# Spilled activations at every fourth step of the loop over v; the routing's low parts on VectorE, and three expert tiles a turn in its last turns

## The chip, the core and the metric

The kernel runs on one core of a Trainium2 chip. The metric is the device time of one launch in microseconds; the times shown of the kernel before are three runs. The engines: TensorE (PE; PEld its weight loads), VectorE (DVE), ScalarE (ACT), GpSimd (POOL) and SyncE (SP), which issues most transfers. Each engine works through its own queue in order and waits on semaphores for the others.

## The reference

One layer of a hybrid block on 512 tokens of width 1024, all in float32: two token mixers run side by side and are merged into x, then an expert network (PEER) is added, then a last norm. The change touches only the expert network:

```python
q = (tok @ w_q).reshape(n_tok, 8, 2, 128)          # 8 heads, 2 halves
s = einsum('nhpc,hpkc->nhpk', q, sub_keys)         # 128 keys per half
s_top, i_top = top_k(s, 16)
cand = s_top[:, :, 0, :, None] + s_top[:, :, 1, None, :]
best, pos = top_k(cand.reshape(n_tok, 8, 256), 16) # expert = 128 * i + j
gate = softmax(best)
act = gelu(einsum('tkd,td->tk', u[expert], tok)) * gate
out = einsum('tk,tkd->td', act, v[expert])         # 128 experts a token of 16384
```

## The kernel before

The first 128 tokens fetch the rows of u and v that they chose by indirect DMA (`gather`), 128 rows of u and 128 of v; each landed row is one VectorE instruction over 128 x 1024 (`dotu`, then `addv`). The other 384 tokens are done densely: h = gelu(u x) for all 16384 experts, in 128 expert tiles of 128 experts, times a routing weight W that is zero for the experts not chosen, then the product with v. Matrix products are made in three passes (lines 93 to 95): an operand is split into a high part (ScalarE, line 98) and a low part, source minus high part (line 99), by `split`, whose argument `sub` names the engine of the low part.

The order of all of it is written out in the code; there is no planner. A tile of weights goes through `Tiles`: `load` (DMA), `split`, then the matmuls. `H` makes one expert tile: it loads and splits ahead (`feed`: load three tiles ahead, split two ahead), runs 24 matmuls of 384 columns and applies gelu. The first 30 expert tiles (`SPILL`) are written out to DRAM (`dA`) from a ring of three buffers, the next 37 (`AHEAD`) stay in SBUF, and the last 61 are made in the loop over v, into buffers that it has freed.

The stages from 560 us on:

1. Routing, turns n = 0 to 20. A turn makes query tile n (n < 16; `q_mm`, 24 matmuls of 512 columns), its low part (`q_lo`), the scores of half n - 1 (`s_mm`), one to two expert tiles (`H`), the two best-16 searches of half n - 2 (`top_keys`, VectorE), and drives `pairs`, a generator that for each head finds the 16 best of 50 candidate sums and turns their places into expert numbers (VectorE, with the sums on GpSimd); it has five parts, two a turn. `fly` issues gathers for known experts and `land` takes the oldest in. Low parts of query and expert tiles (`wl`) are made by GpSimd here, in the same queue as the candidate sums and the gathers.
2. Transposes of the result, then the W stage: 24 groups, each with four VectorE instructions (`onehot`), 32 matmuls, one landed gather and, in 23 of them, an expert tile. Six more expert tiles follow.
3. The loop over v, steps j = 0 to 127, with 18 matmuls of 512 columns each. `v_load`, `w_load` (every fourth step) and `a_load` (an activation read back from `dA`) issue transfers on SyncE; `v_split` multiplies the activation by W and splits both operands one step ahead. In the first 30 steps every activation is read back and no expert tile is made; from step 30 on each step makes one, until step 90. `pace` spreads the gathers that are left by weights of 11.0 a step, 3.5 less for a step that reads back and 16.5 for an expert tile. Loading of expert tiles beyond the 67th is held back by `cap` during the first steps.

The lines on which the argument turns:

```python
for _ in range(2 if n > 12 else 1 + n % 2):   # expert tiles of turn n, behind s_mm
    H()
...
if hn < NK and hn - AHEAD <= j:               # expert tile in step j over v
    H()
w_load(j + 2)
a_load(j + 2)                                 # if j + 2 < SPILL
```

Of the kernel before, what the change touches and what calls it, by code (L numbers as in the profile page):

```python
# [8 lines left out]
FT = mybir.dt.float32  # L9
# [4 lines left out]
AF = mybir.ActivationFunctionType  # L14
# [11 lines left out]
NK = 128  # L26
# [47 lines left out]
def hybrid_block(ctx: ExitStack, tc: tile.TileContext, A, out, dbg=None):  # L74
    nc = tc.nc
    dbg = dbg or {}
# [62 lines left out]
    with ExitStack() as fr:  # L139
# [425 lines left out]
        for src, dst in ((ig, aT), (F0, eT)):  # L565
            ps = sm.tile([128, TB, 4], FT, name="s")
# [197 lines left out]
    ND = T - NS  # L764
    AHEAD = 37
    NA = 22
    SPILL = dbg.get('spill', 30)
# [2 lines left out]
    TAIL = NK - AHEAD + 8  # L770
    GSCALE = 2.0 ** 14
    RES = dbg.get('res', 6)
    EARLY = dbg.get('early', (1, 1))
    fin = ctx
    fin.enter_context(tc.manual_schedule())
    dA = dram.tile([SPILL, 128, ND], FT, name="dA")
# [3 lines left out]
    iota = pe.tile([128, 128], FT, name="iota")  # L780
# [8 lines left out]
    wqr = pool(rs_, "wqr", 3, reuse_waits="tile")  # L789
# [18 lines left out]
                split(self.f.pop(i), h, l, self.sub)  # L808
                self.p[i] = h, l

    WQ = Tiles((wqr, wqr, wqr), A["w_q_t"], 16, nc.gpsimd, 2)
    qs = {}

    def q_half(n, c, ps):
        h, l = WQ.p[n]
        cs = slice(c * 256, (c + 1) * 256)
# [13 lines left out]

    WQ.load(0)
    WQ.load(1)
    WQ.load(2)
    nc.sync.dma_start(tok0, bcast(A["norm2_row"], D))
    WQ.split(0)
    WQ.split(1)
    first = [rps.tile([128, T], FT, name="q") for _ in range(2)]
# [15 lines left out]
    rings = [pool(fin, "ring" + x, 3, side="right", reuse_waits="tile") for x in "fhl"]  # L853
    ring = pool(fin, "ring", 3, side="right", reuse_waits="tile")
    acts = [pool(fin, "actA", NA, side="right", reuse_waits="tile")]
    U = Tiles(rings, A["u_t"], NK, nc.gpsimd)
    act = {}
    hn = 0

    cap = [AHEAD + SPILL] * 2  # L860
    fed = [3, 2]

    def feed(i):

        while fed[0] < min(cap[0], NK, i + 4):
            U.load(fed[0])
            fed[0] += 1
        while fed[1] < min(cap[1], NK, i + 3):
            U.split(fed[1])
            fed[1] += 1  # L870

    def H():

        nonlocal hn
        i = hn
        hn += 1
        feed(i)
        h, l = U.p.pop(i)
        ps = hps.tile([128, ND], FT, name="h")
        for k in range(KD):  # L880
            mm3(ps, h[:, k], l[:, k], th[:, k, NS:], tl[:, k, NS:], k == 0, k == KD - 1)
        if i < SPILL:
            a = ring.tile([128, ND], FT, name="as", bufs=3)
            nc.scalar.activation(a, ps, AF.Gelu)
            nc.sync.dma_start(dA[i], a)
        else:
            act[i] = acts[(i - SPILL) % AHEAD // NA].tile([128, ND], FT, name="act")
            nc.scalar.activation(act[i], ps, AF.Gelu)  # L888


    def gather(src, j, pl):
# [26 lines left out]
    def land(n):  # L918
        for _ in range(n):
            if flying:  # L920
                f, j, t, pl = flying.pop(0)
                f(j, t)
                room.append(pl)
# [51 lines left out]
    def q_lo(n):  # L975
        ps, qh = qs[n]
        ql = rtt.tile([128, T], FR, name="ql")
        nc.vector.tensor_tensor(ql, ps, qh.bitcast(FT), op=OP.subtract)
        qs[n] = qh, ql
# [101 lines left out]

    U.load(0)
    key_load(0)
    key_load(1)
    U.load(1)
    U.load(2)
    key_split(0)
# [4 lines left out]
    def step():  # L1092
        for g in list(live):
            if next(g, 0) == 0:
                live.remove(g)

    n = 0
    while n < 18 or live:
        WQ.load(n + 3)
        key_load(n + 2)  # L1100
        key_split(n + 1)
        if n < 16:
            q_mm(n)
        WQ.split(n + 2)
        if 1 <= n <= 16:
            s_mm(n - 1)
        for _ in range(2 if n > 12 else 1 + n % 2):
            H()
        t = n - 2
        step()  # L1110
        if 0 <= t < 16:
            top_keys(t, (0, 1))
        fly()
        if n < 16:
            q_lo(n)
        step()
        if 0 <= t < 16:
            top_keys(t, (2, 3))
            if t % 2:
                live.append(pairs(t // 2))  # L1120
        land(EARLY[n % 2])
        n += 1

    flat = lambda t, b: t[:, b].rearrange("p h j -> p (h j)")
# [10 lines left out]
    for n in range(3):  # L1135
        if n == 2:
            H()
        ps = rps.tile([128, ND], FT, name="tr", tag="q" if n % 2 else "s")
# [8 lines left out]
            nc.vector.tensor_tensor(tr[3], gf, tr[2], op=OP.subtract)  # L1147
    nc.vector.tensor_copy(g0, flat(sel[2], 0))
    rs_.close()
    U.sub = nc.vector  # L1150
    acts.append(pool(fin, "actB", AHEAD - NA, reuse_waits="tile"))

    H()
    H()

# [2 lines left out]
    wp = pool(wb, "wb", 1, reuse_waits="tile")  # L1158
    wps = pool(wb, "wps", 5, space=PSUM)
    iota4 = wp.tile([128, 128, 4], HF, name="iota4")  # L1160
    nc.vector.tensor_copy(iota4, iota.unsqueeze(2).to_broadcast([128, 128, 4]))
    GT = 16
    NG = ND // GT
    onehots = {}
# [18 lines left out]
    for g in range(NG):  # L1183
# [9 lines left out]
        for a in range(GT // 4):  # L1193
            ps = wps.tile([128, 4, 128], FT, name="w")
# [32 lines left out]
    def w_load(i):  # L1227
        if i < NK and i % 4 == 0:
            Wt[i // 4] = vp.tile([128, ND // 32, 128], FT, name="W", bufs=2)
            nc.sync.dma_start(Wt[i // 4], dW[i // 4].rearrange("g p x -> p g x"))  # L1230

    def a_load(i):
        if i < SPILL:
            act[i] = ring.tile([128, ND], FT, name="as", bufs=3)
            nc.sync.dma_start(act[i], dA[i])

    def v_split(i):
        if i < NK:
# [18 lines left out]
    PV, PS, PH = dbg.get('pace', (11.0, 3.5, 16.5))  # L1257
# [29 lines left out]
    while hn < AHEAD + SPILL:  # L1287
        H()
        if hn == AHEAD + SPILL - 3:
            v_load(0)  # L1290
            a_load(0)
            w_load(0)
            v_load(1)
            a_load(1)
            nc.sync.dma_start(acc, x1[0:128, :])
        if hn == AHEAD + SPILL - 1:
            v_split(0)
        if hn < AHEAD + SPILL - 2:
            land(1)
            fly()  # L1300
    room.extend([gp] * 3)
    fly()
    xts = {0: acc}
    loaded, parted = 2, 1
    for j in range(NK):
        w = PV - PS * (j < SPILL)
        if SPILL - 12 <= j < SPILL and j % 3 == SPILL % 3:
            cap[0] += 1
            cap[1] += j > SPILL - 12
            feed(hn - 1)  # L1310
        if j == SPILL:
            cap = [NK] * 2
        if hn < NK and hn - AHEAD <= j:
            H()
            w += PH
        while loaded < min(NK, j + (3 if j < TAIL + 3 else 4)):
            v_load(loaded)
            loaded += 1
        w_load(j + 2)
        a_load(j + 2)  # L1320
        while parted < min(NK, j + (2 if j < TAIL + 6 else 3)):
            v_split(parted)
            parted += 1
        pace(w / 2)
        if j < NK - LAST:
            for b in range(ND // 128):
                for c in range(2):
                    VV(j, b, c)
            vparts.pop(j)
        pace(w / 2)  # L1330
        n = j - (NK - 10)
        if n == 0:
            assert not todo and not flying
            nc.sync.dma_start(tok0, bcast(A["final_g"], D))
        if 1 <= n < TB:
            xts[n] = (gp if n == 3 else ga).tile([128, D], FT, name="gat", bufs=3 if n == 3 else 2)
            nc.sync.dma_start(xts[n], x1[n * 128:(n + 1) * 128, :])
# [58 lines left out]
```

## Time and profile before

| | |
|---|---|
| median of three runs | 1892.53 us (1892.1 to 1897.6) |
| profiled execution | 1887.46 us, span 1885.7 us |
| mean granted clock of TensorE | 0.983 |
| TensorE busy | 1805.1 us, 96% |
| VectorE, ScalarE, GpSimd busy | 1372.3, 738.6, 559.3 us |
| transfers | 431.40 MB, mean 229 GB/s |

A busy time is the union of an engine's instructions in a stretch; a matmul's shown duration overlaps that of the next, so the time from one start to the next is what a matmul takes. The stages lie at about 566 to 851 us (routing), 851 to 870 (transposes), 870 to 1062 (W), 1062 to 1082 (six expert tiles), 1082 to 1217 (first 30 steps over v), 1217 to 1717 (steps with expert tiles), and 1717 to the end.

### The profile page before, as it was taken

The page shows a single profiled execution, that of the slowest core. Times are in us where ns is not written, and L with a number is a line of the kernel's source. Part 1 is how long each engine was busy: PE and PEld are TensorE (multiplying, and loading weights), DVE is VectorE, ACT ScalarE, POOL GpSimd, SP SyncE. Part 2 cuts the span into 40 slices and gives each one's busy share as a digit, 9 for nine tenths or more (in the row PEclk, how much of TensorE's full clock was granted, in tenths as well). Part 3 has the DMA queues.
Part 4 walks back from the last instruction along what each step waited for, and adds up shares of the span by engine and source line. Part 5 has one row for each costly group of instructions (what it writes and reads, how often), then busy time and mean ns, then how long its engine had stood idle before and what let it go on. Part 6 is the DMA issues. An engine that isn't in the chain of part 4 may idle for free.

```text
span 1885.7 us, 27396 instructions
## 1 busy us (share of the span) xinstructions
PE 1805.1 (96%) x10281; PEld 1590.1 (84%) x10281; DVE 1372.3 (73%) x2559; ACT 738.6 (39%) x1099; POOL 559.3 (30%) x498
## 2 busy tenths in 40 slices
PE   7999899999999998988999999999999999999998
PEld 6777678887879988888999977899999999998886
DVE  6576673554653799989888476678778877877975
ACT  4565433554334323224444433333333333332433
POOL 0000011100216556462222211155454444444500
PEclk9999999999999999989999999999999999999999
DMA  4446455335625443355888998889999999898982
GB/s 156 133 148 194 134 196 173 113 102 180 228 101 164 150 149 122 126 167 176 270 264 263 307 303 304 301 307 326 323 328 332 325 314 338 310 324 282 374 278 71
DMA packets 242502, 431.40 MB, mean 229 GB/s; under 512 B 22976, under 2 KB 149568, under 8 KB 241344
## 3 DMA queue, kind: packets, MB, share of 16 engines
q1 hardware_dynamic: 143088, 257.66, 40.6%
q0 software_dynamic: 36864, 134.23, 20.5%
q10 hardware_dynamic: 62416, 37.75, 6.7%
q8 instruction: 81, 1.33, 0.3%
q14 instruction: 53, 0.43, 0.1%
HBM read 372.83 MB, written 56.75 MB: 228 GB/s over the span
## 4 chain that ended last, share of the span: by engine, by line
PE 59%; DVE 11%; DMA 4%; issue 1%; ACT 1%; POOL 1%; SPq 0%; DVEq 0%; ACTq 0%; POOLq 0%
PE po L93 8%; PE h L93 8%; PE h L95 8%; PE h L94 8%; PE po L94 8%; PE po L95 8%; PE w L1197 5%; DMA as<-dA 2%; PE m L95 1%; PE m L93 1%; PE m L94 1%; DVE vl L99 1%; DMA vf<-in_v_dram 1%; DVE mr L1001 1%; DVE gat L898 1%
## 5 line engine op out<-in xcount | busy, mean ns | idle before, releaser
L95 PE MATMUL h<-th,wl 128*128 128x384 f32 x1024 | 347.5, 339 | 8.0 <-POOL wl L99 8.0
L93 PE MATMUL h<-tl,wh 128*128 128x384 f32 x1024 | 350.8, 343 | 0.0
L94 PE MATMUL h<-th,wh 128*128 128x384 f32 x1024 | 347.1, 339 | 0.0
L893 POOL DMA_INDIRECT gat<-in_u_dram,eid x128 | 174.8, 1365 | 393.0 <-DVE gat L898 378.9
L93 PE MATMUL po<-vl,ah 128*128 128x512 f32 x654 | 256.9, 393 | 9.0 <-DVE vl L99 9.0
L98 ACT ACTIVATE wh<-wf 128x1024 fp32r<-128x1024 f32 x208 | 218.8, 1053 | 103.2 <-PE m L94 83.0
L94 PE MATMUL po<-vh,ah 128*128 128x512 f32 x654 | 256.2, 392 | 0.0
L95 PE MATMUL po<-vh,al 128*128 128x512 f32 x654 | 255.7, 391 | 0.0
L893 POOL DMA_INDIRECT gat<-in_v_dram,eid x128 | 186.4, 1456 | 209.6 <-DVE acc L904 184.0
L99 DVE TENSOR_TENSOR wl<-wf,wh 128x1024 fp32r<-128x1024 f32 x154 | 188.1, 1222 | 60.7 <-ACT wh L98 60.4
L99 DVE TENSOR_TENSOR vl<-vf,vh 128x1024 fp32r<-128x1024 f32 x111 | 135.9, 1225 | 122.5 <-ACT vh L98 122.1
L888 ACT ACTIVATE act<-h 128x384 f32<-128x384 f32 x98 | 48.2, 492 | 433.1 <-PE h L95 433.1
L95 PEld LDWEIGHTS h<-th,wl 128*128 128x128 f32 x1024 | 195.3, 191 | 8.7 <-POOL wl L99 8.7
L93 PEld LDWEIGHTS h<-tl,wh 128*128 128x128 f32 x1024 | 196.1, 192 | 2.4
L94 PEld LDWEIGHTS h<-th,wh 128*128 128x128 f32 x1024 | 195.8, 191 | 2.3
L99 POOL TENSOR_TENSOR wl<-wf,wh 128x1024 fp32r<-128x1024 f32 x54 | 132.9, 2472 | 112.6 <-ACT wh L98 112.4
L904 DVE SCALAR_TENSOR_TENSOR acc<-gat,dots,acc 128x1024 f32<-128x1024 f32 x128 | 164.1, 1282 | 2.4
L95 PE MATMUL m<-hh,wl 128*128 128x512 f32 (+1 forms) x392 | 154.9, 395 | 9.3 <-DVE wl L99 9.3
L898 DVE SCALAR_TENSOR_TENSOR gat<-gat,tok 128x1024 f32<-128x1024 f32 x128 | 160.0, 1274 | 3.8 <-DMA gat<-in_u_dram,eid 3.8
L93 PE MATMUL m<-hl,wh 128*128 128x512 f32 (+1 forms) x392 | 154.2, 393 | 5.4 <-DVE hl L99 4.2
L94 PE MATMUL m<-hh,wh 128*128 128x512 f32 (+1 forms) x392 | 153.4, 391 | 0.0
L93 PEld LDWEIGHTS po<-vl,ah 128*128 128x128 f32 x654 | 123.4, 189 | 35.5 <-ACT ah L98 11.4
(390 smaller groups left out, 3262.7 us busy)
## 6 DMA issues: line engine op xcount, KB each, us to landing
wf<-in_u_t_dram SPq DMA_DIRECT2D x128, 512.0 KB
vf<-in_v_dram SPq DMA_DIRECT2D x111, 512.0 KB
W<-dW SPq DMA_DIRECT2D x32, 768.0 KB
wf<-in_w_in_t_dram SPq DMA_DIRECT2D x46, 512.0 KB
dW<-stg ACTq DMA_DIRECT2D x11, 2048.0 KB
wf<-in_v_dram SPq DMA_DIRECT2D x17, 512.0 KB
wf<-in_w_q_t_dram SPq DMA_DIRECT2D x16, 512.0 KB
dA<-as SPq DMA_DIRECT2D x30, 192.0 KB
```

The source lines that it names most:

```text
L93: nc.tensor.matmul(ps, lh, rl, start=first, stop=False)
L94: nc.tensor.matmul(ps, lh, rh, start=False, stop=False)
L95: nc.tensor.matmul(ps, ll, rh, start=False, stop=last)
L98: nc.scalar.activation(hi, src, AF.Copy)
L99: (sub or nc.vector).tensor_tensor(lo, src, hi.bitcast(FT), op=OP.subtract)
L888: nc.scalar.activation(act[i], ps, AF.Gelu)
L893: nc.gpsimd.indirect_dma_start(out=t, out_offset=None, in_=src, in_offset=bass.IndirectOffsetOnAxis(ap=eid[:, j:j + 1], axis=0))
L898: nc.vector.scalar_tensor_tensor(t, t, 1.0, tok0, op0=OP.mult, op1=OP.mult, accum_out=dots[:, j:j + 1])
L904: nc.vector.scalar_tensor_tensor(acc, t, dots[:, j:j + 1], acc, op0=OP.mult, op1=OP.add)
L1001: nc.vector.match_replace(r[x], m[:, 0:8], v, -3.0e38)
L1197: nc.tensor.matmul(ps[:, r], og[k][:, a, :, r], O1[:, a, :, r], start=k == 0, stop=k == 1)
```

## The change

Five edits. Query and expert low parts are made on VectorE in the routing too. A turn of the routing makes its expert tiles ahead of the score step instead of behind it, three of them in turns 16 to 20 instead of two; the query's low part comes ahead of the first best-16 search; and no gather is taken in after turn 12. The spilled expert tiles are 0, 4, 8, ..., 116 (`early`) instead of 0 to 29: the expert tiles are made in the order `horder`, the spilled ones first. In the loop over v expert tiles start at step 1 and are spread evenly over 90 steps (`ready`), as far as buffers have been freed; W and activations are loaded three steps ahead instead of two, and `cap` goes. One cast (`iota4`) goes to GpSimd.

```diff
-    WQ = Tiles((wqr, wqr, wqr), A["w_q_t"], 16, nc.gpsimd, 2)
+    WQ = Tiles((wqr, wqr, wqr), A["w_q_t"], 16, nc.vector, 2)
...
-    U = Tiles(rings, A["u_t"], NK, nc.gpsimd)
+    early = [4 * i for i in range(SPILL)]
+    horder = early + [i for i in range(NK) if i not in early]
+    U = Tiles(rings, [A["u_t"][i] for i in horder], NK, nc.vector)
...
-        while fed[0] < min(cap[0], NK, i + 4):
+        while fed[0] < min(NK, i + 4):
...
-            act[i] = acts[(i - SPILL) % AHEAD // NA].tile([128, ND], FT, name="act")
+            a = act[horder[i]] = acts[(i - SPILL) % AHEAD // NA].tile([128, ND], FT, name="act")
...
+        for _ in range(3 if n > 15 else 2 if n > 12 else 1 + n % 2):
+            H()
         if 1 <= n <= 16:
             s_mm(n - 1)
-        for _ in range(2 if n > 12 else 1 + n % 2):
-            H()
         t = n - 2
         step()
+        if n < 16:
+            q_lo(n)
         if 0 <= t < 16:
             top_keys(t, (0, 1))
         fly()
-        if n < 16:
-            q_lo(n)
         step()
...
-        land(EARLY[n % 2])
+        if n < 13:
+            land(1)
...
-    nc.vector.tensor_copy(iota4, iota.unsqueeze(2).to_broadcast([128, 128, 4]))
+    nc.gpsimd.tensor_copy(iota4, iota.unsqueeze(2).to_broadcast([128, 128, 4]))
...
-        if i < SPILL:
+        if i in early:
             act[i] = ring.tile([128, ND], FT, name="as", bufs=3)
-            nc.sync.dma_start(act[i], dA[i])
+            nc.sync.dma_start(act[i], dA[i // 4])
...
+    rest = [i for i in range(NK) if i not in early]
+    def ready(j):
+        free = sum(i < parted for i in rest)
+        return hn - AHEAD - SPILL < min(free, (j + 1) * (NK - AHEAD - SPILL) / (NK - AHEAD - 1))
     for j in range(NK):
-        w = PV - PS * (j < SPILL)
-        if SPILL - 12 <= j < SPILL and j % 3 == SPILL % 3:
-            cap[0] += 1
...
-        if hn < NK and hn - AHEAD <= j:
+        w = PV - PS * (j in early)
+        if hn < NK and ready(j):
             H()
...
-        w_load(j + 2)
-        a_load(j + 2)
+        w_load(j + 3)
+        a_load(j + 3)
```

How instructions move, at the places of which the prediction speaks. On VectorE, from the head of turn 7 of the routing; `kl` is the low part of the keys, `wl` that of a query or expert tile, `ge` to `qr` a part of `pairs`. Before, then now:

```order
L99 TENSOR_TENSOR kl<-kw,kh 128x128
L1040 TENSOR_TENSOR ge<-pf,st_5130 128x1024
L1043 TENSOR_TENSOR ge<-ge,dl_5750 128x1024
L1045 TENSOR_REDUCE v<-ge 128x64
L1052 TENSOR_TENSOR vi<-v,i_5747 128x64
```

```order
L99 TENSOR_TENSOR kl<-kw,kh 128x128
L99 TENSOR_TENSOR wl<-wf,wh 128x1024 x3
L1041 TENSOR_TENSOR ge<-pf,st_5130 128x1024
L1044 TENSOR_TENSOR ge<-ge,dl_6076 128x1024
L1046 TENSOR_REDUCE v<-ge 128x64
```

Three low parts, of one query tile and two expert tiles, now stand at the head of VectorE's turn, ahead of its part of `pairs`; they have left GpSimd's queue.

On ScalarE, from the scores of turn 16 on: `wh` is a high part, `as` and `act` the gelu that closes an expert tile, `sc` the copy of a group of scores. Before, then now:

```order
L989 ACTIVATE sc<-s 128x512
L98 ACTIVATE wh<-wf 128x1024
L884 ACTIVATE as<-h 128x384
L98 ACTIVATE wh<-wf 128x1024
L884 ACTIVATE as<-h 128x384
L98 ACTIVATE wh<-wf 128x1024
L884 ACTIVATE as<-h 128x384
```

```order
L98 ACTIVATE wh<-wf 128x1024
L885 ACTIVATE as<-h 128x384
L98 ACTIVATE wh<-wf 128x1024
L885 ACTIVATE as<-h 128x384
L98 ACTIVATE wh<-wf 128x1024
L885 ACTIVATE as<-h 128x384
L990 ACTIVATE sc<-s 128x512
```

Turn 16 now makes three expert tiles, and its scores follow them; each high part stands behind the gelu of the tile before it.

On SyncE, in the loop over v where activations are read back: `vf` a tile of v, `wf` an expert tile of u, `W` the weights of four tiles, `as` an activation. Before, then now:

```order
L1230 DMA W<-dW 128x12x128
L1235 DMA as<-dA 128x384
L1225 DMA vf<-in_v_dram 128x1024
L1235 DMA as<-dA 128x384
L1225 DMA vf<-in_v_dram 128x1024
L1235 DMA as<-dA 128x384
L1225 DMA vf<-in_v_dram 128x1024
L1235 DMA as<-dA 128x384
```

```order
L1231 DMA W<-dW 128x12x128
L1236 DMA as<-dA 128x384
L801 DMA wf<-in_u_t_dram 128x1024
L1226 DMA vf<-in_v_dram 128x1024
L801 DMA wf<-in_u_t_dram 128x1024
L1226 DMA vf<-in_v_dram 128x1024 x2
L801 DMA wf<-in_u_t_dram 128x1024
L1226 DMA vf<-in_v_dram 128x1024
```

One activation in four steps is read back now, right behind W, and expert tiles of u are loaded between.

## Rows read from the trace of the kernel before

**Rows 1.** The page's first part: busy us (share of the span) and instructions.
```profile
PE 1805.1 (96%) x10281; PEld 1590.1 (84%) x10281; DVE 1372.3 (73%) x2559; ACT 738.6 (39%) x1099; POOL 559.3 (30%) x498
```

**Rows 2.** Busy us by stage: PE, PEld, DVE, ACT, POOL; PE clock, DMA, GB/s.
```profile
566.00:630.00 64.00, 62.86 (x361) 58.12 (x361) 24.05 (x129) 25.15 (x41) 36.72 (x58) 1.00 0.49 160
630.00:751.00 121.00, 112.12 (x587) 103.04 (x587) 118.38 (x489) 39.16 (x62) 73.23 (x69) 0.96 0.44 143
751.00:851.00 100.00, 89.06 (x466) 86.51 (x465) 91.06 (x356) 27.10 (x38) 53.15 (x53) 0.90 0.45 143
870.00:1062.00 192.00, 191.50 (x1346) 186.56 (x1347) 162.16 (x166) 93.05 (x144) 38.81 (x24) 0.99 0.82 253
1062.00:1082.00 20.00, 20.00 (x118) 20.00 (x117) 9.37 (x13) 6.57 (x10) 6.37 (x6) 1.00 1.03 353
1082.00:1217.00 135.00, 127.40 (x545) 103.38 (x545) 93.56 (x139) 49.23 (x64) 22.34 (x22) 0.97 0.90 304
1217.00:1717.00 500.00, 500.00 (x2545) 458.16 (x2544) 394.99 (x469) 166.19 (x239) 239.09 (x164) 1.00 0.92 320
```

**Rows 3.** Timeline of TensorE in the routing: start us, us, engine, line, operation, tiles.
```profile
698.62 0.39 PE L93 MATMUL q<-tl,wh 128*128 128x512 f32 x1
704.19 0.22 PE L93 MATMUL s<-kl,qh 128*128 128x128 f32 x1
705.48 0.39 PE L93 MATMUL h<-tl,wh 128*128 128x384 f32 x1
```

**Rows 4.** Timeline of TensorE in the loop over v.
```profile
1407.07 0.34 PE L93 MATMUL h<-tl,wh 128*128 128x384 f32 x1
1411.25 0.39 PE L93 MATMUL po<-vl,ah 128*128 128x512 f32 x1
1415.33 0.34 PE L93 MATMUL h<-tl,wh 128*128 128x384 f32 x1
```

**Rows 5.** Timeline of TensorE: first query matmul of turn 5, first transpose.
```profile
623.73 0.39 PE L93 MATMUL q<-tl,wh 128*128 128x512 f32 x1
...
851.03 0.49 PE L1140 MATMUL tr<-ident,sel 128*128 128x128 f32 x3
```

**Rows 6.** Timeline of TensorE: first step over v, first expert tile after it.
```profile
1082.51 0.39 PE L93 MATMUL po<-vl,ah 128*128 128x512 f32 x1
...
1216.93 0.34 PE L93 MATMUL h<-tl,wh 128*128 128x384 f32 x1
```

**Rows 7.** Groups by line, 630-851 us: count | busy us, mean ns | idle.
```profile
L99 POOL TENSOR_TENSOR wl<-wf,wh 128x1024 fp32r<-128x1024 f32 x37 | 92.3, 2503 | 80.1 <-ACT wh L98 80.0
...
L1052 DVE TENSOR_TENSOR vi<-v,i 128x64 int32<-128x64 f32 x8 | 11.2, 1396 | 0.3
...
L1043 DVE TENSOR_TENSOR ge<-ge,dl 128x1024 f16<-128x1024 f16 x8 | 7.6, 952 | 0.3
```

**Rows 8.** The page's costliest groups: low parts on VectorE.
```profile
L99 DVE TENSOR_TENSOR wl<-wf,wh 128x1024 fp32r<-128x1024 f32 x154 | 188.1, 1222 | 60.7 <-ACT wh L98 60.4
```

**Rows 9.** Timeline of GpSimd and of VectorE at 696 us.
```profile
696.23 2.40 POOL L99 TENSOR_TENSOR wl<-wf,wh 128x1024 fp32r<-128x1024 f32 x1 [3.81 <-ACT wh L98]
...
696.32 2.39 DVE L1052 TENSOR_TENSOR vi<-v,i 128x64 int32<-128x64 f32 x1
```

**Rows 10.** Instructions by tile: duration ns shortest/median/longest, first and last start.
```profile
L1052 DVE TENSOR_TENSOR vi<-v,i x8: 224/1194/3689, 638.5 to 846.2; 128x64 int32<-128x64 f32 x8
...
L1043 DVE TENSOR_TENSOR ge<-ge,dl x8: 691/692/2773, 636.5 to 844.2; 128x1024 f16<-128x1024 f16 x8
```

**Rows 11.** Waits, 630-851 us: us in total, times, longest us.
```profile
DVE best L997 <- POOL cand L1018: 7.1, 3, 4.0
```

**Rows 12.** Chain of waits at the routing's end: start us, us, what.
```profile
852.06 1.23 DVE sel L1045
```

**Rows 13.** Waits, 1082 to 1217 us.
```profile
DVE as L1242 <- DMA as<-dA: 31.0, 16, 6.0
```

**Rows 14.** Chain of waits, 1082 to 1217 us: the longest of five such pieces.
```profile
1159.10 10.29 DMA as<-dA
```

More of the change, by code (lines that the diff above doesn't have):

```diff
@@ L772, in hybrid_block @@
     RES = dbg.get('res', 6)
-    EARLY = dbg.get('early', (1, 1))
     fin = ctx
@@ L855, in hybrid_block @@
     acts = [pool(fin, "actA", NA, side="right", reuse_waits="tile")]
-    U = Tiles(rings, A["u_t"], NK, nc.gpsimd)
+    early = [4 * i for i in range(SPILL)]
+    horder = early + [i for i in range(NK) if i not in early]
+    U = Tiles(rings, [A["u_t"][i] for i in horder], NK, nc.vector)
     act = {}
     hn = 0
-    cap = [AHEAD + SPILL] * 2
     fed = [3, 2]
     def feed(i):
-        while fed[0] < min(cap[0], NK, i + 4):
+        while fed[0] < min(NK, i + 4):
             U.load(fed[0])
             fed[0] += 1
-        while fed[1] < min(cap[1], NK, i + 3):
+        while fed[1] < min(NK, i + 3):
             U.split(fed[1])
@@ L886, in H @@
         else:
-            act[i] = acts[(i - SPILL) % AHEAD // NA].tile([128, ND], FT, name="act")
-            nc.scalar.activation(act[i], ps, AF.Gelu)
+            a = act[horder[i]] = acts[(i - SPILL) % AHEAD // NA].tile([128, ND], FT, name="act")
+            nc.scalar.activation(a, ps, AF.Gelu)
     def gather(src, j, pl):
@@ L1149, in hybrid_block @@
     rs_.close()
-    U.sub = nc.vector
     acts.append(pool(fin, "actB", AHEAD - NA, reuse_waits="tile"))
@@ L1293, in hybrid_block @@
             v_load(1)
-            a_load(1)
             nc.sync.dma_start(acc, x1[0:128, :])
@@ L1304, in hybrid_block @@
     loaded, parted = 2, 1
+    rest = [i for i in range(NK) if i not in early]
+    def ready(j):
+        free = sum(i < parted for i in rest)
+        return hn - AHEAD - SPILL < min(free, (j + 1) * (NK - AHEAD - SPILL) / (NK - AHEAD - 1))
     for j in range(NK):
-        w = PV - PS * (j < SPILL)
-        if SPILL - 12 <= j < SPILL and j % 3 == SPILL % 3:
-            cap[0] += 1
[L1309 to L1312, printed above, removed]
-        if hn < NK and hn - AHEAD <= j:
+        w = PV - PS * (j in early)
+        if hn < NK and ready(j):
             H()
```

## Prediction

> **What bounds the kernel now.** I read the page's first part, then the busy times by stage, then the stages in which TensorE is not full. TensorE is busy for 1805.1 of 1885.7 us [rows 1], so an edit can only give back time in which TensorE waits or runs at its lower clock. The table by stage [rows 2] shows where that is. From 870 to 1062 us (the stage that builds W) it is busy for 191.50 of 192 us, and from 1217 to 1717 us (the loop over v with expert tiles) for all 500. It is not full in two places. From 630 to 851 us, the routing, it has 112.12 of 121 and 89.06 of 100 us, at a granted clock of 0.96 and 0.90, while VectorE has 118.38 of 121 and 91.06 of 100: VectorE sets the pace there. From 1082 to 1217 us, the first 30 steps over v, it has 127.40 of 135 us, with DMA at 0.90 and 304 GB/s.
>
> How much is to be had there I count in tiles. Undisturbed, a query tile (24 matmuls) takes 704.19 - 698.62 = 5.57 us and a group of scores 705.48 - 704.19 = 1.29 us [rows 3]; an expert tile takes 1411.25 - 1407.07 = 4.18 us and a step over v 1415.33 - 1411.25 = 4.08 us [rows 4]. From the query tile of turn 5 to the first transpose 851.03 - 623.73 = 227.3 us pass [rows 5]. In them are 11 query tiles (61.3), 12 groups of scores (15.5) and 28 expert tiles (117.0): 193.8 us of work, 33.5 us lost, the slower clock included. The 30 steps over v take 1216.93 - 1082.51 = 134.4 us [rows 6] for 30 x 4.08 = 122.4: 12.0 us lost. So some 45 us at most.
>
> **Low parts from GpSimd to VectorE.** One low part takes GpSimd 2503 ns [rows 7] and VectorE 1222 ns [rows 8]. Turns 5 to 20 hold 9 of query tiles and 33 of expert tiles (two ahead of the tile, 35 + 5 tiles in the routing): 42 x 1.222 = 51.3 us more for the engine that is full. Three things go.
> First, stalls. At 696.23 us GpSimd starts a low part, and a VectorE instruction on 64 columns that starts 0.09 us later takes 2.39 us and ends with it [rows 9]; the same instruction takes 0.224 us at its fastest [rows 10]. Count times (mean - fastest) is 8 x (1396 - 224) = 9.4 us for this group, the largest, and 8 x (952 - 691) = 2.1 us for the smallest counted [rows 7, 10]; over the eight groups of such two-input instructions and casts from 630 to 851 us it is 42 us. The Trainium skill (SBUF — State Buffer, Who interferes with whom) says that a VectorE instruction with two SBUF inputs and a GpSimd one that reads SBUF share a port, and that the second waits until the first is done; the trace agrees, 2.39 against 0.224 us. I let 38 of the 42 us go, since GpSimd keeps its short sums. Second, landed gathers: after turn 12 none is taken, 8 fewer than before; over the same 1024 columns I price one like a low part, 8 x 1.22 = 9.8 us. Third, VectorE waited 7.1 us for sums that stood behind low parts in GpSimd's queue [rows 11]. Net: 51.3 - 38 - 9.8 - 7.1 = -3.6 us for VectorE. The ends: no stall goes, +34; all go, -8. I take -3.6, by the one pair that is seen to start and end together.
>
> In turns 0 to 4 the added low parts, about 14 x 1.22 = 17 us, fall where VectorE has 24.05 of 64 us busy [rows 2]: nothing, and 1 us at most to gain, since TensorE has 62.86 of 64. The first two stand ahead of a residual add that waits for TensorE's sums: nothing, or 2.4 us if that wait is shorter than they are. The one cast that goes to GpSimd is worth 0 to 0.4 us; I take 0.
>
> **Five more expert tiles in the last turns.** They bring 5 x 4.18 = 20.9 us of work into the stage that has lost time, out of the stage that has none. But they now need VectorE: low parts are made two tiles ahead, so the third tile of a turn waits for the low part at the head of VectorE's own turn, behind its whole turn before. VectorE comes into turn 16 more than a turn behind, so I expect one wait of about 10 us there, with the short ones after it. The end is worked out from VectorE: its last marks ended at 852.06 + 1.23 = 853.3 us [rows 12]; now 3.6 earlier, and 3.7 earlier because the three low parts of turn 20 come after them: 846.0. At the heads of turns 17 to 20 VectorE in turn waits for high parts that ScalarE makes only when the second tile of the turn is done: +3. Then the low part of the last tile (1.2), and the tile (4.2): 854.4. TensorE has waited and gets its clock back late, as in the stretch at 0.90 now: +3. The first transpose starts at 857 instead of 851, with 20.9 us less left to do: **-15 us**. The ends: -28 if hardly anything is lost, +23 if the stalls stay (a rival).
> Query and score steps change places too, and the low part of the query comes ahead of the first top-k. That gives the score step more lead; it is inside the estimate.
>
> **The W stage** keeps 24 groups but 18 tiles instead of 23. TensorE: 191.5 - 20.9 = 170.6 us. VectorE: 162.16 [rows 2] - 5 x 1.22 = 156. TensorE stays the bound with half of its margin gone: +1 (0 to +8).
>
> **Spilled tiles 0, 4, ..., 116 instead of 0 to 29.** In the 30 steps VectorE waits 31.0 us for activations read back, in 16 waits, and the chain has five pieces of that kind, the longest 10.29 us [rows 13, 14]. The load was issued at step j for j + 2 and is wanted one step, 4.08 us, later. Now it is issued for j + 3, wanted two steps later, and a mean step with 61 tiles over 90 steps takes 4.08 + 0.68 x 4.18 = 6.9 us: 14 us of lead against 10. The waits go unless DMA as a whole can't follow. Bytes: 304 x 135 us + 320 x 500 us = 201 MB [rows 2]; 7 of the 8 late gathers add 7 x 0.52 = 3.7 MB, and the time falls from 635 to some 622 us: 329 GB/s. At 320 GB/s (share 0.92) TensorE lost nothing, and from 1062 to 1082 us 353 GB/s were moved. I leave 2.5 us lost: **-9.5 us** (-12 to +1). The gathers' VectorE time, 10 us, is covered: 394.99 of 500 busy.
> In the last 37 steps, without expert tiles, 7 spilled tiles now stand. Steps are 4.08 us there, so the lead is 8.2 us, and half of that for the last three, against a landing of up to 10.29: +2 (0 to +10).
>
> **Sum.** -15 + 1 - 9.5 + 2 = -21.5 us. The profiled execution took 1887.46 us, which gives 1866.0; the median of the three runs shown is 5.1 us above it, so 1871.0.
>
> **Rivals.**
> *VectorE becomes the bound of the routing, slower than before.* Rows 2 speak for it: 98% busy already, and 42 instructions are added. If the stalls are something else than GpSimd's low parts, all 38 us stay: -21.5 + 38 = +16.5, 1909. It ends on the other side once more than 21.5 of the 38 us stay. Against it stand the two rows that end together [rows 9]. The Trainium skill (Perfetto Trace Analysis, Optimizing Scalar/DVE Operations) advises giving work of a saturated VectorE to ScalarE or GpSimd, the reverse of this edit, and adds that the shared port may spoil it; here the trace bears out the second half. 0.10.
> *The loop over v gains nothing*, because DMA at 0.95 of its time comes late elsewhere: the 12 us stay. -15 + 1 + 0 + 2 = -12, 1880.5; with the gathers' 4.2 MB at 320 GB/s (13 us) fully paid it is no change. For it: the share. Against: 353 GB/s in rows 2. 0.17.
> *The routing loses hardly anything*: VectorE sheds the whole 42 us and stays within a turn. -28 + 0 - 11 + 1 = -38, 1854.5. 0.18.
> *The five tiles only wait*: each third tile waits as long as it works, so the idle time moves and isn't filled. -15 becomes 0: -6.5, 1886. 0.08.
>
> **How the numbers follow.** The forecast has 0.47, by itself 1862 to 1880. A measurement can tell about 0.3%, 5.7 us, from no change. Faster: 0.47 + 0.18, 0.13 of the 0.17 and 0.03 of the 0.08: 0.81. Within 0.3%: 0.04 + 0.03 and 0.02 from the edges: 0.09. Slower: 0.10. The range leaves out most of the slow rival and the far half of the fast one: 1852 to 1888.
>
> **What will show it.** In the profile after: VectorE's 64-column instruction near 0.22 us throughout; the first transpose at 852 to 862 us with 40 expert tiles before it; one long wait of TensorE at the third tile of turn 16; W stage some 171 us; no wait of note for activations read back in the first 120 steps; DMA near 329 GB/s. I am wrong if VectorE's stalls stay, if the transposes come after 870 us, or if TensorE idles all through the loop over v.

## The result and the profile after

The changed kernel takes 1866.11 us (median of 4 runs, 1861.26 to 1869.28), the kernel before 1893.32 on the same chip (4 runs, 1892.1 to 1897.6): a ratio of 0.985, interval 0.9823 to 0.9877, or 27 us less. The profiled execution took 1865.59 us, against 1887.46 before: 21.9 us less, where the sum had 21.5.

The page's first part of the kernel after, to be held against [rows 1]: busy us, share of the span, instructions.

```profile
span 1863.8 us, 27416 instructions
...
PE 1796.7 (96%) x10281; PEld 1583.1 (85%) x10281; DVE 1380.5 (74%) x2612; ACT 740.0 (40%) x1099; POOL 461.6 (25%) x445
```

TensorE has as many instructions as before. GpSimd lost 98 us of work, and VectorE, which took it over, has only 8 us more. The table by stage, cut at the bounds as they lie now (busy us of PE, PEld, DVE, ACT, POOL; clock, DMA share, GB/s), answers to [rows 2]:

```profile
630.00:751.00 121.00, 119.70 (x647) 109.40 (x646) 117.48 (x512) 42.89 (x66) 31.04 (x48) 0.99 0.46 150
751.00:859.00 108.00, 95.89 (x526) 93.11 (x525) 91.45 (x360) 30.16 (x42) 18.88 (x32) 0.95 0.36 120
876.00:1067.00 191.00, 191.00 (x1341) 186.80 (x1342) 162.78 (x168) 90.06 (x140) 45.21 (x30) 0.99 0.88 277
1067.00:1082.00 15.00, 10.53 (x47) 9.14 (x47) 9.28 (x12) 6.65 (x9) 1.68 (x1) 0.89 0.97 332
1082.00:1217.00 135.00, 135.00 (x674) 121.69 (x673) 105.70 (x158) 47.22 (x66) 63.12 (x43) 1.00 0.92 320
1217.00:1695.00 478.00, 478.00 (x2367) 429.19 (x2366) 382.70 (x455) 165.49 (x232) 223.06 (x152) 1.00 0.93 326
```

Of the stretches that lost time, TensorE now nearly fills 630 to 751 us (119.70 of 121) and wholly fills 1082 to 1217 us. 751 to 859 us still has 12 us in which TensorE waits. And from 1067 to 1082 us there is a gap that the kernel before didn't have. The bounds themselves, TensorE's timeline of the kernel after (start us, us; in brackets the idle time ahead):

```profile
623.02 0.45 PE L93 MATMUL q<-tl,wh 128*128 128x512 f32 x1
...
858.96 0.38 PE L1142 MATMUL tr<-ident,sel 128*128 128x128 f32 x2
...
875.92 0.65 PE L1198 MATMUL w<-O,Og 128*128 128x128 f16 x4 [3.29 <-DVE O L1179]
...
1067.51 0.34 PE L95 MATMUL h<-th,wl 128*128 128x384 f32 x1
1072.31 0.76 PE L93 MATMUL po<-vl,ah 128*128 128x512 f32 x1 [4.47 <-DVE vl L99]
```

With [rows 5, 6] and the same starts of before (first W matmul 870.5, last expert matmul 1082.3, last matmul over v 1876.7; after 1855.8) the 21.9 us come apart as follows; "turn 5" is the first matmul of its query tile, as in the prediction.

- start to turn 5: -0.7
- turn 5 to the first transpose: 227.3 to 235.9, +8.6, with 20.9 us more work in it
- to the first W matmul: 19.5 to 17.0, -2.5
- to the last expert tile ahead of the loop: 211.8 to 191.6, -20.2, with 20.9 us less work in it
- to the first step over v: 0.2 to 4.8, +4.6
- the steps over v, first to last matmul: 794.2 to 783.5, -10.6
- the end: -1.1

By the prediction's terms: routing -15.5 (forecast -15), W stage +0.7 (+1), everything after it -7.1 (-9.5 + 2). The routing's -15.5 is counted to the first W matmul; to the first transpose, which is where the prediction's sum for it ends, it is -13.0.

VectorE's stalls are gone. The tile view of the kernel after (shortest/median/longest ns, first and last start), against [rows 10]:

```profile
L1053 DVE TENSOR_TENSOR vi<-v,i x8: 224/225/227, 638.4 to 847.8; 128x64 int32<-128x64 f32 x8
```

TensorE's waits from 630 to 860 us, after (us in total, times, longest); VectorE's longest from 630 to 859 us; and ScalarE's gelu that closes the third tile of turns 16, 17 and 18:

```profile
PE h L95 <- DVE wl L99: 12.1, 4, 5.8
PE s L95 <- DVE ql L979: 1.3, 1, 1.3
```

```profile
DVE wl L99 <- ACT wh L98: 13.7, 6, 3.2
```

```profile
803.09 0.49 ACT L885 ACTIVATE as<-h 128x384 f32<-128x384 f32 x1 [11.35 <-PE h L95]
...
816.89 0.49 ACT L889 ACTIVATE act<-h 128x384 f32<-128x384 f32 x1 [2.40 <-PE h L95]
...
834.19 0.49 ACT L889 ACTIVATE act<-h 128x384 f32<-128x384 f32 x1 [7.55 <-PE h L95]
```

The wait for a low part at turn 16 that the prediction named is there: its three tiles (12.5 us of work) take from 780.2 to 802.8 us, 22.7 us, 10 of them lost: TensorE waits 6.9 us in them, and its granted clock from 780 to 804 us is 0.86. Turn 17's third tile doesn't wait, turn 18's does (2.9 us), and the twelve tiles of turns 17 to 20 lose 4.7 us in all. In the steps over v the 31.0 us of [rows 13] have left the list; VectorE's one wait from 1082 to 1217 us is now another, and costs TensorE nothing, which is busy for all 135 us:

```profile
DVE vl L99 <- ACT vh L98: 32.7, 14, 5.1
```

### The profile page after: what moved, and what is told of

It reads as the page before. It is cut to its first block, busy times and chain, and to the rows that moved or that the text cites. A ratio compares the mean times of both kernels' runs of the same rounds, so it can differ in the third digit from the quotient of the medians.

```text
span 1863.8 us, 27416 instructions
## 1 busy us (share of the span) xinstructions
PE 1796.7 (96%) x10281; PEld 1583.1 (85%) x10281; DVE 1380.5 (74%) x2612; ACT 740.0 (40%) x1099; POOL 461.6 (25%) x445
## 4 chain that ended last, share of the span: by engine, by line
PE 53%; issue 10%; DVE 9%; DMA 3%; POOL 2%; ACT 1%; SPq 0%; DVEq 0%; POOLq 0%; ACTq 0%
PE po L93 9%; PE po L94 9%; PE po L95 9%; PE h L95 6%; PE h L93 6%; PE h L94 6%; POOL gat L894 2%; DVE wl L99 1%; PE m L95 1%; PE m L93 1%; PE m L94 1%; DMA vf<-in_v_dram 1%; DVE mr L1002 1%; PE q L93 1%; PE q L94 1%
## 5 line engine op out<-in xcount | busy, mean ns | idle before, releaser
L95 PE MATMUL h<-th,wl 128*128 128x384 f32 x1024 | 345.6, 338 | 12.1 <-DVE wl L99 12.1
L99 DVE TENSOR_TENSOR wl<-wf,wh 128x1024 fp32r<-128x1024 f32 x208 | 252.2, 1223 | 107.8 <-ACT wh L98 107.6
L894 POOL DMA_INDIRECT gat<-in_u_dram,eid x128 | 191.5, 1496 | 381.1 <-DVE gat L899 318.0
L98 ACT ACTIVATE wh<-wf 128x1024 fp32r<-128x1024 f32 x208 | 217.3, 1052 | 108.4 <-PE m L94 78.3
L95 PEld LDWEIGHTS h<-th,wl 128*128 128x128 f32 x1024 | 193.8, 189 | 13.9 <-DVE wl L99 13.8
L899 DVE SCALAR_TENSOR_TENSOR gat<-gat,tok 128x1024 f32<-128x1024 f32 x128 | 152.2, 1220 | 4.1 <-DMA gat<-in_u_dram,eid 4.1
L98 ACT ACTIVATE vh<-vf 128x1024 fp32r<-128x1024 f32 x111 | 117.1, 1055 | 86.6 <-issue 38.4
```

Of the source, the lines that this page charges most:

```text
L95: nc.tensor.matmul(ps, ll, rh, start=False, stop=last)
L98: nc.scalar.activation(hi, src, AF.Copy)
L99: (sub or nc.vector).tensor_tensor(lo, src, hi.bitcast(FT), op=OP.subtract)
L894: nc.gpsimd.indirect_dma_start(out=t, out_offset=None, in_=src, in_offset=bass.IndirectOffsetOnAxis(ap=eid[:, j:j + 1], axis=0))
L899: nc.vector.scalar_tensor_tensor(t, t, 1.0, tok0, op0=OP.mult, op1=OP.mult, accum_out=dots[:, j:j + 1])
```

## Experiments

Times are medians; the experiments ran on four chips, and before ran beside each on the same chip, at 1893 to 1894 us. The table has the routing's stages of the profiled executions, from the starts in TensorE's timeline, as for before and after above. "To W" is turn 5 to the first W matmul, less 20.9 us where five more expert tiles lie in it, so that all rows hold the same work.

| kernel | tiles | low parts | turn 5 to transpose | to W, same work | median |
|---|---|---|---|---|---|
| before | 35 | GpSimd | 227.3 | 246.8 | 1893.3 |
| before, landings ended | 35 | GpSimd | 211.9 | 233.7 | 1877.8 |
| and new order (two tiles) | 35 | GpSimd | 208.1 | 229.4 | 1866.9 |
| and third tiles | 40 | GpSimd | 226.9 | 223.0 | 1858.8 |
| after, two tiles | 35 | VectorE | 217.3 | 234.2 | 1865.7 |
| after | 40 | VectorE | 235.9 | 232.0 | 1866.1 |

Rows 3 to 6 have the change's loop over v as well; the first two don't. Row 3 adds the new order to row 2, and row 4 the third tiles to row 3. How far such stage times repeat, runs with the same routing code show: 235.9, 235.6 and 235.1 us up to the transpose (after, splits held, routing alone), 226.9 and 225.3 (row 4, both repairs). The profiled execution of a kernel, from which they come, lay up to 6 us off the median of its runs.

**Each half alone.** First the routing's edits on the kernel before:

```
-    WQ = Tiles((wqr, wqr, wqr), A["w_q_t"], 16, nc.gpsimd, 2)
+    WQ = Tiles((wqr, wqr, wqr), A["w_q_t"], 16, nc.vector, 2)
...
+        for _ in range(3 if n > 15 else 2 if n > 12 else 1 + n % 2):
+            H()
...
+        if n < 13:
+            land(1)
```

> The routing's edits alone, the loop over v as before. If the routing gives what the trace of the changed kernel shows at the end of the W stage (15 us), the median falls by 13 to 17 us against before, and the loop's 12 lost us stay. Rival, that the gain is the evened transfers alone: within 4 us of before. Rival, that the two parts need each other (the evened loop's demand hides a gain or a loss): this gain and that of the spread alone do not add up to 22 us within 5.

1877.08 us, ratio 0.9897 (0.9857 to 0.9937): 17 us. Then the spill order, the queueing and the release of the loop over v alone:

```
+    early = [4 * i for i in range(SPILL)]
...
-    cap = [AHEAD + SPILL] * 2
...
+        a_load(j + 3)
```

> The spread of the spilled tiles alone, the routing as before. The 12 us lost in the first 30 steps go, and the wait of 4.8 us at the first step, which the trace of the changed kernel shows behind expert tiles split ahead of the first tile of v, comes: 6 to 9 us faster than before. Rival, that the wait comes from the earlier end of the W stage (the written W not yet back): no wait at the first step, 11 to 13 us faster.

1880.79 us, 0.9926 (0.9903 to 0.9948): 13 us, above the 6 to 9 expected. The two sum to 30 against 27 together; within the runs' spread they add. (The 22 us that the first expectation names is the difference of the two profiled executions; by it the two would not add.) The gap at the first step over v (5 us) is in the second and not in the first: the spill edit brings it.

**Low parts back on GpSimd**, in the routing alone, all else as after:

```
-    WQ = Tiles((wqr, wqr, wqr), A["w_q_t"], 16, nc.vector, 2)
+    WQ = Tiles((wqr, wqr, wqr), A["w_q_t"], 16, nc.gpsimd, 2)
```

> The changed kernel with the routing's low parts back on GpSimd, all else as changed. My sum has the 51 us of low parts on VectorE nearly paid by stalls and waits that end (net -3.6): the stalls return, and the median stays within 6 us of the changed kernel, either way. Rival, that the end of the stalls is the gain itself: the routing's 15 us are lost, 12 to 18 us slower than the changed kernel. Rival, that low parts on VectorE hurt, since third tiles wait for them: 6 to 15 us faster than the changed kernel.

1858.82 us (1856.68 to 1862.37), ratio to before 0.9813 (0.9775 to 0.985): 7.3 us faster than the changed kernel. The two ratios' intervals overlap; the same edit on the kernel with the splits held (below) gives 9.0 us, the same way. The stalls come back, as this tile view says, and TensorE loses less all the same:

```profile
L1053 DVE TENSOR_TENSOR vi<-v,i x8: 224/225/1549, 639.7 to 836.7; 128x64 int32<-128x64 f32 x8
```

Its stretch from 751 us to the first transpose (columns as above):

```profile
751.00:849.00 98.00, 98.00 (x567) 95.82 (x566) 92.18 (x378) 33.07 (x48) 57.84 (x52) 1.00 0.41 141
```

No tile waits for a low part there, and TensorE is busy for all 98 us. GpSimd is slow at a low part, 2430 ns, but it is free for one early: it waits 45.2 us in all for ScalarE's high parts (630 to 849 us). On VectorE the low part stands behind a turn.

```profile
L99 POOL TENSOR_TENSOR wl<-wf,wh 128x1024 fp32r<-128x1024 f32 x42 | 101.4, 2430 | 46.2 <-ACT wh L98 45.2 <-DMA wf<-in_u_t_dram 0.9
```

**Two tiles in turns 16 to 20**, all else as after:

```
-        for _ in range(3 if n > 15 else 2 if n > 12 else 1 + n % 2):
+        for _ in range(2 if n > 12 else 1 + n % 2):
```

> The changed kernel with two expert tiles instead of three in turns 16 to 20. If the tiles fill time in which TensorE would wait, five tiles (20.9 us) go back to the W stage and the first transpose comes only some 9 us earlier (850 instead of 859 us): 8 to 14 us slower than the changed kernel. Rival, that the third tiles wait as long as they work: the first transpose comes 20 us earlier, no change within 4 us.

1865.73 us (1863.45 to 1871.31): the same as with three. Five tiles, 20.9 us of work, lengthen the routing by 18.7. TensorE's waits for low parts stay nearly as they were (740 to 860 us of this kernel), while VectorE waits only 1.9 us for high parts (630 to 842 us), where it waits 13.7 with three tiles:

```profile
PE h L95 <- DVE wl L99: 13.9, 4, 5.2
```

```profile
DVE wl L99 <- ACT wh L98: 1.9, 2, 1.0
```

**Gathers landed in every turn**, all else as after:

```
-        if n < 13:
-            land(1)
+        land(1)
```

> The changed kernel with a gather landed in every turn, also after turn 12. If VectorE sets the routing's pace through turn 17, 8 more instructions of 1.22 us push the first transpose back by 6 to 10 us, and 5 to 10 us are lost against the changed kernel. Rival, that the waits of the last turns hide them: within 3 us, and up to 2 us faster since the loop over v has 8 gathers less.

1874.42 us (1869.46 to 1876.49): 8 us lost, 4.4 of them ahead of the first transpose.

**Is it GpSimd's reading that stalls VectorE?** Two kernels, each run once, have a needless GpSimd instruction after every low part of the changed routing: one that reads a 128x1024 tile twice, one that only writes such a tile.

```
+                    nc.gpsimd.tensor_tensor(junk, h, h, op=OP.subtract)
```

> The changed kernel, with one more GpSimd subtraction of 128 x 1024 for each low part of the routing, into a tile that nobody reads. If GpSimd's reads hold VectorE up, VectorE's 64-column instruction (0.22 us) goes over 1 us on average again, the routing has some 40 us of stalls on top of the 51 us of low parts, and the first transpose comes 25 to 45 us later. Rival, that the stalls had another cause (VectorE's waits, DMA): all stays at 0.22 us and the time within 6 us.

```
+                    nc.gpsimd.memset(junk, 0.0)
```

> The changed kernel, with one more GpSimd fill of 128 x 1024 (no read) for each low part of the routing. If two-input VectorE instructions are held up only by a GpSimd instruction that reads, the 64-column instruction stays at 0.22 us and the first transpose within 5 us of the changed kernel's 859. Rival, that any GpSimd instruction holds VectorE up: it goes over 0.5 us on average and the transpose comes 10 us later or more.

Reading: 1898.49 us, 32 more than after, and the routing to the first transpose 268.2 against 235.9. Writing: 1869.44, and 237.6. The groups of the needless instruction, reading and writing, and VectorE's 64-column instruction of each:

```profile
L810 POOL TENSOR_TENSOR junk<-wh 128x1024 f32<-128x1024 f32 x42 | 89.5, 2130 | 60.0 <-ACT wh L98 58.8
```

```profile
L1058 DVE TENSOR_TENSOR vi<-v,i x8: 224/226/703, 642.6 to 880.8; 128x64 int32<-128x64 f32 x8
```

```profile
L810 POOL MEMSET junk<- 128x1024 f32 x38 | 36.5, 959 | 1.6
```

```profile
L1058 DVE TENSOR_TENSOR vi<-v,i x8: 224/225/227, 641.3 to 852.4; 128x64 int32<-128x64 f32 x8
```

The stall of over 1 us on average that was expected of this very instruction didn't come with the reads. It fell on others; for example, a group of the instructions that mark ranks (`ge`) took 1822 ns a piece instead of 692 (the same kernel, 630 to 860 us):

```profile
L1049 DVE TENSOR_TENSOR ge<-ge,dl 128x1024 f16<-128x1024 f16 x7 | 12.8, 1822 | 0.2
```

Over all of VectorE's groups from 630 us to the transposes, count times (mean - shortest) is 41.4 us with the reads and 7.8 in the changed kernel: 34 us more, about what the stage lost. So the reads cost 32 us up to the first transpose; the writes, 36.5 us of GpSimd's time, cost 1.7, close to what the stage repeats to.

**The splits of expert tiles 67 and on held** until the first rows of v are split, all else as after:

```
+    hold = [AHEAD + SPILL]
...
-        while fed[1] < min(NK, i + 3):
+        while fed[1] < min(NK, hold[0], i + 3):
...
+        if j == 0:
+            hold[0] = NK
+            feed(hn - 1)
```

> The changed kernel, but expert tiles beyond the 67th are split only after the first two tiles of v are. If the wait of 4.8 us before the first step over v comes from VectorE standing behind the split of an expert tile whose load lands late, it goes: 4 to 6 us faster than the changed kernel. Rival, that the first step waits for the weights W or for transfers as such: no change, the wait moves to another name.

1860.3 us (1855.96 to 1865.55), ratio 0.9829 (0.9789 to 0.9868): 5.8 us less than after, with intervals that overlap; the same edit on the kernel with low parts on GpSimd gives 7.5 us (below). What stood there in the changed kernel, in its chain of waits, in VectorE's timeline and in its waits from 1060 to 1080 us:

```profile
1059.03 10.42 DMA wf<-in_u_t_dram
```

```profile
1059.20 1.22 DVE L99 TENSOR_TENSOR wl<-wf,wh 128x1024 fp32r<-128x1024 f32 x1
1069.34 1.23 DVE L99 TENSOR_TENSOR wl<-wf,wh 128x1024 fp32r<-128x1024 f32 x1 [8.91 <-ACT wh L98]
1070.48 0.55 DVE L1243 TENSOR_TENSOR as<-as,W 128x384 f32<-128x384 f32 x1
1070.95 1.22 DVE L99 TENSOR_TENSOR vl<-vf,vh 128x1024 fp32r<-128x1024 f32 x1
```

```profile
DVE wl L99 <- ACT wh L98: 8.9, 1, 8.9
ACT wh L98 <- DMA wf<-in_u_t_dram: 8.2, 1, 8.2
```

The change took out `cap`, which had kept tiles 67 and on from being loaded and split before the loop. Without it the low part of such a tile stands in VectorE's queue ahead of the first product with W and the first low part of v, and it waits 8.9 us, since ScalarE's high part waits 8.2 us for the tile's weights (the chain has a load of 10.42 us there). With the splits held, TensorE goes from the last expert tile to the first step without a wait:

```profile
1063.90 0.34 PE L95 MATMUL h<-th,wl 128*128 128x384 f32 x1
1064.08 0.39 PE L93 MATMUL po<-vl,ah 128*128 128x512 f32 x1
```

**What the routing's gain is made of.** Three more kernels. Two tiles in turns 16 to 20 where GpSimd makes the low parts (the edit of the two tiles, on the kernel with low parts back on GpSimd):

```
+        for _ in range(2 if n > 12 else 1 + n % 2):
```

> Low parts of the routing on GpSimd and two expert tiles in turns 16 to 20 instead of three. Theory: the third tiles are worth nothing in the changed kernel because their low parts stand in VectorE's queue behind a whole turn; with GpSimd making them they fill time in which TensorE waits. Then the routing with 35 tiles takes nearly as long as the 226.9 us of 40 tiles: 218 to 224 us from turn 5 to the first transpose, and the kernel loses 12 to 18 us against three tiles, 1871 to 1877. Rival: third tiles are worth nothing wherever the low parts are made; then 206 us, and 1859 as with three. What lies between the two cases shares the 18 us.

1866.92 us (1864.39 to 1869.2), 208.1 us ahead of the first transpose: the rival's 206 there, and yet 8 us slower than with three tiles in all. Here TensorE waits, and its clock is lower, behind the routing:

```profile
832.00:853.00 21.00, 15.37 (x81) 14.78 (x80) 13.87 (x22) 7.15 (x9) 2.97 (x2) 0.90 0.28 100
```

With GpSimd the third tiles fill 6.4 us up to the first W matmul (table), with VectorE 2.2. With two tiles the place of the low parts makes no difference by the medians (1866.9 with GpSimd, 1865.7 with VectorE), though the table's stage is 4.8 us shorter with GpSimd. Then the old order, with three tiles and GpSimd:

```
-        for _ in range(3 if n > 15 else 2 if n > 12 else 1 + n % 2):
-            H()
         if 1 <= n <= 16:
             s_mm(n - 1)
+        for _ in range(3 if n > 15 else 2 if n > 12 else 1 + n % 2):
+            H()
```

> Low parts of the routing on GpSimd, three tiles in the last turns, gathers landed to turn 12 as in the changed kernel, but scores ahead of the expert tiles and the query's low part behind the first top-k, as in the kernel before. Theory: the changed order gives ScalarE and VectorE the time of a tile to make the query ready for its scores, and is worth about 6 us over the 12 turns (TensorE waits for ql in nearly every turn without it): 1865, 233 us from turn 5 to the first transpose. Rival: order is worth nothing, since VectorE sets the pace and its work is the same: 1859, 227 us.

1862.7 us (1861.89 to 1864.32) against 1858.8: the order is worth 3.9 us, between the 6 and the 0 that were expected; in the stage up to the transpose it is worth 3.8 (230.7 against 226.9). And the kernel before with nothing but the end of the landings:

```
-        land(EARLY[n % 2])
+        if n < 13:
+            land(1)
```

> The kernel before with one edit: no gather is landed after turn 12. From turn 5 to the first transpose it took 227.3 us; with this edit, the new order, and low parts on GpSimd still, the same 35 tiles took 208.1 (two tiles in the last turns). This run splits those 19.2 us between landings and order. Theory: VectorE sets the pace, so the eight landings are worth their time on it, 8 x 1.22 = 9.8: 217.5 us, and 1884 for the kernel. Rival: they are worth what putting them back into the changed kernel cost, 4.3: 223 us, 1889. Second rival: with GpSimd reading beside them each landing is also stalled, and they are worth the 15.3 that are left when the 3.9 of the order, as it was measured with 40 tiles, is taken off: 212 us, 1878.

1877.79 us (1873.51 to 1881.57), ratio 0.9907 (0.9874 to 0.994), 211.9 us ahead of the transpose: the second rival's number. This one edit gives 16 us by the medians, as much as the whole routing (1877.08); the two profiled executions differ by 5.9 us only, as before's lay under its median and this one's over. Of the eight landings six had come ahead of the first transpose. VectorE's landings from 630 to 851 us, before and then without the late ones, and the wait that one of the late gathers took part in, on GpSimd's and TensorE's timelines of before:

```profile
L898 DVE SCALAR_TENSOR_TENSOR gat<-gat,tok 128x1024 f32<-128x1024 f32 x13 | 20.5, 1576 | 0.0
```

```profile
L898 DVE SCALAR_TENSOR_TENSOR gat<-gat,tok 128x1024 f32<-128x1024 f32 x7 | 10.4, 1483 | 0.0
```

```profile
833.23 2.79 POOL L1016 TENSOR_TENSOR cand<-stop 128x64 f32<-128x64 f32 x8 [8.34 <-DVE stop L1003]
...
836.73 0.97 POOL L893 DMA_INDIRECT gat<-in_u_dram,eid  x1 [0.16 <-DVE best L997]
837.72 4.68 POOL L99 TENSOR_TENSOR wl<-wf,wh 128x1024 fp32r<-128x1024 f32 x2
...
840.13 0.69 PE L95 MATMUL h<-th,wl 128*128 128x384 f32 x1 [7.18 <-POOL wl L99]
```

A landing took 1576 ns here, against 1206 in the kernel after. GpSimd's low parts alone don't do that: in the new order, with them back on GpSimd, it took 1208. The sums and the gather ahead of a low part cost TensorE one wait of 7.18 us, of which 0.8 are left without the late landings.

**Both repairs together**: low parts of the routing on GpSimd and the splits held.

```
+    WQ = Tiles((wqr, wqr, wqr), A["w_q_t"], 16, nc.gpsimd, 2)
...
+        while fed[1] < min(NK, hold[0], i + 3):
```

> The changed kernel with both repairs: the routing's low parts on GpSimd, and the splits of expert tiles 67 and later held until the first rows of v are split. Alone the first gave 1858.8 (7.3 less than the changed kernel) and the second 1860.3 (5.8 less). They lie in different stages (the routing before 860 us, the start of the loop over v). If they add: 1853, first step over v at 1058.5 with no wait, 1.0215 times as fast as before. If the gain of the second was a matter of chance of the clock: 1858.5.

1851.35 us (5 runs, 1848.55 to 1855.14), ratio to before 0.9782 (0.9759 to 0.9806): 14.8 us less than the changed kernel, 42 less than before. TensorE's waits from 630 to 1080 us are two lines:

```profile
PE s L95 <- DVE ql L980: 6.6, 2, 3.5
PE w L1200 <- DVE O L1181: 3.3, 1, 3.3
```

## Why the prediction was right, and where not

**The total** came out as summed, -21.9 against -21.5 of the profiled execution. The 1871 missed the median by 5 us because of the last step alone: before's profiled execution lay 5 us under the median of its runs, after's (1865.59) at it.

**The routing's -15** came out (-15.5) with wrong terms in it whose errors happened to cancel. Up to the first W matmul, by the table:
- The end of the landings: priced 9.8, worth 246.8 - 233.7 = 13.1 there and 16 in the whole kernel. The price fits the landings themselves: VectorE spent 20.5 - 10.4 = 10.1 us less on them (six, at some 1.7 us each). What I left out is what else went with them: the stalls of VectorE's other groups fell from 46.0 to 39.7 us, and TensorE's wait behind a gather and sums from 7.2 to 0.8. Put back into the changed kernel, where GpSimd makes no low parts, the same landings cost 4.4 us up to the transpose.
- The order: "inside the estimate", worth 233.7 - 229.4 = 4.3. The list of waits of before (630 to 851 us) would have let me price it, since TensorE's waits for the low part of the query were there; after, 1.3 us of them are left:

```profile
PE s L95 <- DVE ql L978: 12.6, 6, 4.2
```

- Low parts to VectorE: 51.3 - 38 - 7.1 = +6.2 in the sum, +4.8 with two tiles and +9.0 with three in the runs. The stalls ended as forecast: over VectorE's groups of the routing but the landings, count times (mean - shortest) went from 46.0 to 7.7 us, 38 less for the 38. (The 42 us from which I took the 38 come out only with the landings among the eight groups, 4.9 us; the other seven have 37.6.) The waits for GpSimd's sums went from 7.1 to 0.8. So VectorE's balance was well drawn, and still this edit made the kernel slower, by 7 us with three tiles a turn. With two, the medians show no loss.
- Five tiles: with the transpose forecast at 857 and VectorE 3.6 us earlier than before, they were to fill 20.9 - (857 - 847.4) = 11 us of idle time. They filled 2.2. The step that failed is what comes behind the one wait at turn 16. That wait is there, and the turn loses the 10 us forecast. But third tiles also make VectorE wait, at the heads of its turns, for high parts that ScalarE makes late: I put 3 us for that, and it waits 13.7, against 1.9 with two tiles. Its last marks ended at 850.57 + 1.22 = 851.8 us (below), not at 846.0 + 3. That they came only 3 us later than forecast, and the transposes only 2, is luck: from turn 5 to its last marks VectorE was busy for 3.4 us less than before (211.7 against 215.1), where the sum had it about even (51.3 - 3.7 - 38 - 9.8). So the idle time moved and was hardly filled: TensorE's waits for low parts are 12.1 us with three tiles and 13.9 with two. This was the rival that I gave 0.08, right in what became of the idle time, if not tile by tile (two of the five third tiles wait, three don't), and wrong in its total, since the other edits paid.

```profile
850.57 1.22 DVE L1046 TENSOR_REDUCE sel<-ge 128x64 f32<-128x1024 f16 x1
```


**VectorE as the bound** (0.10) didn't come, since the stalls went; but its mechanism, low parts that load a full VectorE, does cost the routing 4.8 us (two tiles) to 9.0 (three); of the kernel's median it costs 7.3 us with three tiles, and with two nothing that shows. The Trainium skill (Perfetto Trace Analysis, Optimizing Scalar/DVE Operations) says that it may make sense to give some of a saturated VectorE's work to ScalarE or GpSimd, and warns that the shared port may undo it. With three tiles a turn the advice holds in spite of the port: 1858.8 with GpSimd, 1866.1 with VectorE.

**The W stage** went as forecast, 191.6 us with the tiles that follow it, for -20.9 + 1.

**The loop over v.** The first 30 steps lost 12 us and lose 2 now; I had left 2.5. DMA moved 320 to 326 GB/s where I had asked for 329. The steps behind the last expert tile lose 4.5 us, as before, not 2 more. What I missed is 4.6 us ahead of the first step. The prediction has no term for the end of `cap`: its removal put instructions that wait for a transfer ahead of others in VectorE's queue.

**What stays open.** Alone, the spill edit gave 13 us by the medians, while its profiled execution is 5.4 us shorter from the last expert tile to the end (798.0 against 803.4). As wholes the two profiled executions differ by 3.0 us only: before's lay 6 us under the median of the runs beside the experiment, this one's 4 us over its own. In which stage the other executions were longer or shorter, no run here tells. The one cast that goes to GpSimd was not tried by itself, and the third tiles not on the kernel before.

## What to carry to other kernels

A change of several edits that lands on its forecast proves the sum, not the terms: here one edit alone, eight gathers not landed, gave as much as all the routing's edits together, and the edit beside it that looked best reasoned cost 7 us. Count for each moved instruction not just the time on its new engine, but what stands ahead of it there and who waits for its result: with three tiles a turn, the slow engine with an empty queue was the better place. When a limit is taken out, list everything that it held back, and look at the queues in which that now stands first.

## What the runs showed of the hardware

A GpSimd instruction that reads held VectorE's two-input instructions up (32 us for 89.5 us of reading), one that only writes didn't (1.7 us for 36.5 us): VectorE's 64-column instruction took 224/225/227 ns beside it, as without it. The Trainium skill (SBUF — State Buffer, Who interferes with whom) says that a VectorE instruction with two SBUF inputs contends with a GpSimd one that reads SBUF and not with one that only writes it; both runs agree. What I had not expected is that it costs so little of what it could: with 101 us of GpSimd's reading back in the routing, the kernel was the faster one. VectorE's 64-column instruction then takes up to 1549 ns, and TensorE is busy for all 98 us from 751 to 849 us nonetheless.
